# Strassen's scheme for three quarters of an MLP's first product, on one core

## The chip, the core and the metric

The kernel runs on one core of a Trainium2 chip. The core has a matrix engine (TensorE, PE in the profile; PEld is its loading of weights), three engines for elementwise work (VectorE = DVE, ScalarE = ACT, GpSimd = POOL), and SyncE (SP), whose queue issues the DMAs here. Each engine has its own queue of instructions, and semaphores order the work between them. SBUF is the memory that the engines work in, PSUM the one that TensorE writes its products to. The metric is the device time of one execution in microseconds (us); lower is better. Every number below is from the profile of one execution or from the times of the runs.

## The reference

One layer of a decoder: attention and a gated linear recurrence beside each other, merged, then an MLP with a squared ReLU. It is computed for 512 prompt tokens and 64 sample tokens (8 requests of 8), which share the weights; together 576 columns. The part that the change rewrites is the MLP, with D_MODEL = 1024 and D_FF = 4096:

```python
u2 = x1 * (1 + sc2) + sh2
hid = jnp.square(jax.nn.relu(jnp.einsum('bsd,df->bsf', u2, w_up) + b_up))
ff = jnp.einsum('bsf,fd->bsd', hid, w_down) + b_down
x2 = _layer_norm(DN_ALPHA * x1 + g2 * ff, ln2_g, ln2_b, dtype)
```

Everything is float32. The sample tokens have a scale and shift (`sc2`, `sh2`) for each request, the prompt has one.

## The kernel before

**Precision.** TensorE multiplies in a reduced format (fp32r). Each float32 operand is therefore split into a high part, rounded to fp32r by an ACT copy, and a low part, the DVE difference; a product is three matmuls: high by high, high by low, low by high.

**Layout.** Activations lie transposed: 8 pages of 128 channels by 576 columns each. The columns go in two halves of `HF` = 288, each a matmul's moving operand. A block is 128 output channels: for each half, 8 steps of k by 3 terms, so 2 x 24 = 48 matmuls into one PSUM bank per half (`half`, line 1780, with `mm_part`, line 382), then the eviction of that bank.

**Weights.** A unit is 1024 rows by 512 columns (4 blocks) or 256 columns (2 blocks). `load_one` (line 307) loads it in pieces of 1 MB into three raw buffers (`NRAW`); a buffer is handed on by `weights_done`. `split_slot` (line 372) makes the high and low parts of one block, in instructions of 128 x 512: an ACT copy to `whi` and a DVE subtraction to `wlo` for each piece. Token-major units (the values of the attention, the last product of the MLP) are split by rows of k instead, in `split_k` (line 355), 512 columns at a time.

**Pages.** Nearly all of SBUF is one pool of `NPG` = 68 pages of 128 x 576 floats. Activations, weight parts, caches and temporaries all take pages; a page comes free when the last instruction that touches it has run.

**Order.** The program is straight-line. `tc.manual_schedule()` (line 252) leaves each engine the order in which the Python code issues its instructions. `Side` (line 177) interleaves generators of side work ("lanes") with the matmuls: each `pump` runs a step if its lane is ready by the kernel's own planner (`Engine`, line 109).

**The stages.** The front (until about 905 us) computes projections, attention, the recurrence and the branches. Then come the output product with the first layer norm, then the MLP in four quarters of 1024 of the 4096 hidden channels: 8 up blocks (`up_evac`, line 1765: ACT adds the bias and takes the ReLU, POOL squares, ACT writes the high part `hdh`, DVE the low part `hdl`) and 8 down blocks (`down_evac`, line 1805: added into `acc`). The list `seq` (line 1818) holds them in order; quarter 0's first four up blocks run ahead of it beside the layer norm. The loop over `seq` (line 1866) splits the weights of block i + 1, may issue a copy of cache rows (`copy_rows`), then runs block i. In quarter 0's down blocks ACT also scales the residual `hT`; in quarter 2's the sum is added to `hT` (`gated`). Quarter 3 has no down blocks in `seq`: its down product is made token-major by `blocks` and `tiles` (lines 1968 and 1992), after eight `split_k` at the last block. `residual` (line 1843) transposes gates and residual for that stage beside quarter 3's up blocks.

The lines of the loop around which the change is made:

```python
        if i + 1 < len(seq):
            split(*seq[i + 1][:2])
        else:
            for k in range(AHEAD_K):
                split_k(ud[0], k)
        if i >= 8:
            copy_rows()
        for h in range(2):
            half(u, j, xs, h, ev)
```

Of the kernel before, what the change touches and what calls it, by code (L numbers as in the profile page):

```python
# [19 lines left out]
KT = D // 128  # L20
# [31 lines left out]
NPG = 68  # L52
AHEAD_K = 8
# [190 lines left out]
def decoder_step(ctx, tc, I, O):  # L244
# [3 lines left out]
    raw = ctx.enter_context(tc.tile_pool(name="raw", bufs=NRAW))  # L248
    small = ctx.enter_context(tc.tile_pool(name="small", bufs=2))
# [12 lines left out]
    def page(shape, name, dtype=F32):  # L262
        return pages.tile(shape, dtype, name=name, tag="page")

# [72 lines left out]
    def split(u, j):  # L337


        def there():  # L340
            load_more(True)
            return len(u["slots"]) > j // 5 if u["tok"] else loaded(u)
        if not there():
            side.drain(("a", "s"), there)
        assert there()
        if u["tok"]:
            for k in range(j // 5 * 4, j // 5 * 4 + 4):
                split_k(u, k)
            return
        for s in range(len(u["slots"])):  # L350
            split_slot(u, j, s)
        if j == len(u["blocks"]) - 1:
            weights_done(u["slots"])

    def split_k(u, k, eng=V):

        if k in u["w"]:
            return
        load_more(True)
        t = u["slots"][k // 4][2][:, k % 4]  # L360
        w = u["w"][k] = page([128, 512], "whi", F32R), page([128, 512], "wlo", F32R)
        A.activation(w[0], t, AF.Copy)
        eng.tensor_sub(w[1], t, w[0])
        if k % 4 == 3:
            weights_done(u["slots"][k // 4:k // 4 + 1])
# [6 lines left out]
    def split_slot(u, j, s):  # L372
        k0, kk, t = u["slots"][s]
        hi, lo = u["w"].setdefault(j, ([], []))
        for k in range(0, kk, 4):
            src = t[:, k:k + 4, j * 128:(j + 1) * 128]
            hi.append(page([128, 4, 128], "whi", F32R))
            lo.append(page([128, 4, 128], "wlo", F32R))
            A.activation(hi[-1], src, AF.Copy)
            V.tensor_sub(lo[-1], src, hi[-1])  # L380

    def mm_part(w, nk, xs, h, ps, ks):
        hi, lo = w
        seq = [(hi, 0), (hi, 1), (lo, 0)]
        n = 0
        for k in ks:
            for m, (ww, xi) in enumerate(seq):
                PE.matmul(ps, ww[k // 4][:, k % 4], xs[xi][k][:, h * HF:(h + 1) * HF],
                          start=(k == 0 and m == 0), stop=(k == nk - 1 and m == 2))
                n += 1  # L390
                if n % 8 == 0 and n < 3 * len(ks):
                    side.pump(8 * 123.0)
# [1101 lines left out]
    for qd in range(4):  # L1494
        for n0 in (0, 4):
            unit(I["w_up"][0], 0, 8, (qd * 8 + n0) * 128, 512, [None] * 4)
        for n0 in (0, 4) if qd < 3 else (4, 0, 4):
            unit(I["w_down"][0], qd * 1024, 8, n0 * 128, 512, [None] * 4, tok=(qd == 3))
    for u in units:
        for k0 in range(0, u["nk"], 2048 // u["W"]):  # L1500
            load_q.append((u, k0))
# [83 lines left out]
    for j in range(n_early):  # L1585
        done_split.add((id(u0), j))
        split_slot(u0, j, 0)
# [3 lines left out]
    for s in range(4):  # L1591
# [13 lines left out]
        if s == 1:  # L1605
            for j in range(n_early):
                split_slot(u0, j, 1)
# [197 lines left out]
    def down_evac(qd, n):  # L1805
        def evac(hf, ps):
            if qd == 0:
# [3 lines left out]
                A.activation(hv(hT[n], hf), hv(hT[n], hf), AF.Identity, scale=gbl[:, 0, n:n + 1], bias=gbl[:, 1, n:n + 1])  # L1811
            else:
                V.tensor_add(hv(acc[n], hf), ps, hv(acc[n], hf))
                if qd == 2:
                    gated(hT[n], hv(acc[n], hf), hf, 5, n)
        return evac

    seq = []
    for qd in range(4):
        for n in range(8):  # L1820
            if qd == 0 and n < 4:
                continue
            seq.append((mlp[qd * 4 + n // 4], n % 4, U2, up_evac(qd, n)))
        if qd < 3:
            for n in range(8):
                seq.append((mlp[qd * 4 + 2 + n // 4], n % 4, (Hd[0], Hd[1]), down_evac(qd, n)))
# [16 lines left out]
    def residual():  # L1843
# [11 lines left out]
        for c in range(NM // 128):  # L1855
            for e in range(2):
# [5 lines left out]
                yield 436, None  # L1862

    n_down = len(seq) - 8
    ud = mlp[14:17]
    for i, (u, j, xs, ev) in enumerate(seq):
# [4 lines left out]
        if i == n_down:  # L1871
            side.add("p", residual())
        if i + 1 < len(seq):
            split(*seq[i + 1][:2])
        else:
            for k in range(AHEAD_K):
                split_k(ud[0], k)
        if i >= 8:
            copy_rows()
        for h in range(2):  # L1880
            half(u, j, xs, h, ev)
        u["w"].pop(j)
    side.drain()
    U2_hi[:] = U2_lo[:] = [None] * 8
# [83 lines left out]
    def blocks(w, e):  # L1968
        for n in range(4):
            ps = bank([128, NT - NM], "lin")  # L1970
            for k in range(KT):
                if n == 0 and k + AHEAD_K < KT:
                    split_k(w, k + AHEAD_K)
# [11 lines left out]
    def pass_on(u, k, v):  # L1985
# [3 lines left out]
        if k >= KT - AHEAD_K:  # L1989
            split_k(v, k - KT + AHEAD_K)  # L1990

    def tiles(w, e):
        for c in range(NM // 128):
            last = c == NM // 128 - 1

            def before(k):
                if w is ud[1]:
                    if last and k >= 2:
                        w["w"].pop(k - 2)
                    if k % 2 == SPH:  # L2000
                        split_k(ud[2], 4 * c + k // 2, V if c else G)
# [13 lines left out]
    blocks(ud[1], 0)  # L2015
    tiles(ud[1], 0)
# [38 lines left out]
```

## Time and profile before

| | us |
|---|---|
| median of 3 runs (lowest to highest) | 1381.82 (1379.16 to 1386.65) |
| the profiled execution | 1381.52 |
| its span, first to last instruction | 1379.7 |
| quarter 0's down blocks, in the trace | 1000 to 1053 |
| quarter 1: up blocks, down blocks | 1053 to 1104, 1104 to 1155 |
| quarter 2: up blocks, down blocks | 1155 to 1205, 1205 to 1256 |
| quarter 3's up blocks | 1256 to 1309 |
| its down product and the end | 1309 to 1380 |

In rows of groups, a name such as `wlo<-wraw,whi` is the tile written and the tiles read; after it stand the shapes. A time in brackets after a row of the timeline is the idle time of that engine ahead of it, with what ended it. All instructions carry line 173, that of the helper which issues them, so tiles tell them apart. A row of the windows gives, for a stretch of the span, its length, the busy time of each engine with its instructions, the granted clock of TensorE (1.00 is full), the DMA's share and its GB/s.

### The profile page before, as it was taken

The numbers are of one execution on the slowest core, as the hardware profiler recorded it, in microseconds if no ns is written. First come the engines' busy times: TensorE is split into PE (matmuls) and PEld (weight loads), VectorE is DVE, ScalarE is ACT, GpSimd is POOL, SyncE is SP. The second block draws the span as 40 slices with busy tenths as digits, with TensorE's granted clock in tenths as the row PEclk, the third lists the DMA queues.
The fourth block names the chain that finished last, engine by engine and source line by source line (L and its number), as shares of the span: only waits on it lengthen the run. The fifth ranks groups of instructions, "written<-read, shape, count | busy, mean of one in ns | idle before, by whom it ended". The sixth has DMA issues, their size and how long they took to land.

```text
span 1379.7 us, 24690 instructions
## 1 busy us (share of the span) xinstructions
PE 1330.6 (96%) x9624; PEld 1228.2 (89%) x9624; DVE 766.6 (56%) x1572; ACT 469.5 (34%) x1101; POOL 359.9 (26%) x419
## 2 busy tenths in 40 slices
PE   6999999999899999999999999999999999999995
PEld 3899898799778887888899999998999999999994
DVE  2456555558767886566655446547522333354458
ACT  3423333332422232333233441325554422413522
POOL 1242023026417563234344200003500200200205
PEclk9999999999999999999999999999999999999998
DMA  9789899689989977776445223331123633522322
GB/s 295 255 306 341 268 317 339 238 272 324 280 282 285 319 243 242 240 239 199 147 157 170 70 73 112 130 123 62 62 107 129 237 124 147 220 77 91 118 99 69
DMA packets 184520, 269.40 MB, mean 195 GB/s; under 512 B 15756, under 2 KB 92372, under 8 KB 183892
## 3 DMA queue, kind: packets, MB, share of 16 engines
q1 hardware_dynamic: 184404, 267.83, 57.7%
q8 instruction: 76, 1.25, 0.4%
q14 instruction: 40, 0.33, 0.1%
HBM read 210.45 MB, written 74.10 MB: 206 GB/s over the span
## 4 chain that ended last, share of the span: by engine, by line
PE 83%; DVE 6%; DMA 4%; ACT 2%; issue 2%; POOL 2%; SPq 1%; DVEq 0%; POOLq 0%; ACTq 0%
PE lin L173 68%; PE att L173 7%; PE tr L173 4%; PE sx L173 4%; DVE wlo L173 2%; DMA out_dram<-kv 2%; DVE res L173 1%; DMA kv<-in_cache_kv_w_dram 1%; POOL qb L173 1%; ACT whi L173 1%; SPq L173 1%; DMA xtm<-in_x_prompt_dram 0%; DMA wraw<-in_w_ada_dram 0%; DMA qb<-qsc 0%; DVE st L173 0%
## 5 line engine op out<-in xcount | busy, mean ns | idle before, releaser
L173 DVE TENSOR_TENSOR wlo<-wraw,whi 128x512 fp32r<-128x512 f32 x340 | 248.4, 774 | 128.5 <-ACT whi L173 125.7
L173 PE MATMUL lin<-uh,whi 128*128 128x288 f32 x992 | 298.4, 301 | 4.3 <-DVE hso L173 2.4
L173 PE MATMUL lin<-uh,wlo 128*128 128x288 f32 x992 | 298.2, 301 | 2.3 <-DVE wlo L173 2.3
L173 PE MATMUL lin<-ul,whi 128*128 128x288 f32 x992 | 299.3, 302 | 1.0 <-DVE ul L173 0.9
L173 ACT ACTIVATE whi<-wraw 128x512 fp32r<-128x512 f32 x344 | 193.4, 620 | 112.8 <-DMA wraw<-in_w_down_dram 29.7
L173 PEld LDWEIGHTS lin<-ul,whi 128*128 128x128 f32 x992 | 187.6, 189 | 13.7 <-issue 10.9
L173 PEld LDWEIGHTS lin<-uh,whi 128*128 128x128 f32 x992 | 187.5, 189 | 10.3 <-DVE hso L173 2.7
L173 PEld LDWEIGHTS lin<-uh,wlo 128*128 128x128 f32 x992 | 187.7, 189 | 7.1 <-issue 3.8
L173 POOL TENSOR_TENSOR qb<-qb,kv 128x512 f32<-128x512 f32 x96 | 128.3, 1356 | 204.0 <-DMA qb<-qsc 90.7
L173 PE MATMUL lin<-u2h,whi 128*128 128x288 f32 x496 | 147.1, 297 | 1.2 <-ACT u2h L173 1.2
L173 PE MATMUL lin<-u2l,whi 128*128 128x288 f32 x496 | 147.0, 296 | 0.3 <-DVE u2l L173 0.3
L173 PE MATMUL lin<-u2h,wlo 128*128 128x288 f32 x496 | 146.8, 296 | 0.0
L173 PE MATMUL lin<-hdh,whi 128*128 128x288 f32 (+1 forms) x448 | 133.6, 298 | 0.2 <-ACT hdh L173 0.2
L173 PE MATMUL lin<-hdl,whi 128*128 128x288 f32 (+1 forms) x448 | 132.9, 297 | 0.1
L173 PE MATMUL lin<-hdh,wlo 128*128 128x288 f32 (+1 forms) x448 | 133.0, 297 | 0.0
L173 POOL TENSOR_TENSOR rel<-rel 128x288 f32<-128x288 f32 x56 | 38.3, 684 | 292.7 <-ACT rel L173 287.7
L173 PEld LDWEIGHTS lin<-u2h,whi 128*128 128x128 f32 x496 | 93.4, 188 | 1.8 <-ACT u2h L173 1.5
L173 PEld LDWEIGHTS lin<-u2l,whi 128*128 128x128 f32 x496 | 93.3, 188 | 1.5 <-DVE u2l L173 0.9
L173 DVE TENSOR_TENSOR hdl<-rel,hdh 128x288 fp32r<-128x288 f32 x61 | 28.4, 466 | 118.5 <-ACT hdh L173 118.5
L173 PEld LDWEIGHTS lin<-u2h,wlo 128*128 128x128 f32 x496 | 93.3, 188 | 0.5 <-issue 0.5
L173 PEld LDWEIGHTS lin<-hdh,whi 128*128 128x128 f32 x448 | 84.1, 188 | 0.7 <-ACT hdh L173 0.4
L173 PEld LDWEIGHTS lin<-hdl,whi 128*128 128x128 f32 x448 | 84.1, 188 | 0.3 <-DVE hdl L173 0.3
(358 smaller groups left out, 2546.6 us busy)
## 6 DMA issues: line engine op xcount, KB each, us to landing
wraw<-in_w_in_dram SPq DMA_DIRECT2D x42, 1024.0 KB
kv<-in_cache_kv_w_dram SPq DMA_DIRECT2D x144, 256.0 KB
qb<-qsc SPq DMA_DIRECT2D x96, 256.0 KB
wraw<-in_w_down_dram SPq DMA_DIRECT2D x18, 1024.0 KB
out_dram<-kv SPq DMA_DIRECT2D x64, 256.0 KB
wraw<-in_w_ada_dram SPq DMA_DIRECT2D x16, 1024.0 KB
wraw<-in_w_up_dram SPq DMA_DIRECT2D x16, 1024.0 KB
out_dram<-in_cache_kv_w_dram SPq DMA_DIRECT2D x32, 512.0 KB
```

The lines of the kernel that those rows point to most:

```text
L173: return f(out, *args, **kw)
```

## The change

A unit of `w_up` (1024 rows by 512 columns) is taken as 2 x 2 blocks A11, A21, A12, A22 of 512 rows by 256 columns, and the input u2 as 2 x 2 blocks of 512 channels by 288 columns. Strassen's scheme, in Winograd's form, makes the product from seven products of such blocks or of sums of them, in place of eight. This is done in quarters 1, 2 and 3; quarter 0's up blocks and all down blocks stay as they are.

- `input_sums` makes the sums of the inputs and their high and low parts once, as side work beside quarter 0's down blocks; it also stores `hT` to DRAM (`xsc`) and gives up its pages. `reload` brings `hT` back beside quarter 2's down blocks, where its scaling now stands too.
- `seven` gives a unit's seven products as pairs of `prep(f)` (the sum of weights on DVE, in place in the raw buffer, for four of them; a high part on ACT and a low part on DVE, each of 128 x 1024) and `run(f)` (two column groups of 12 matmuls, the eviction with bias or the DVE addition of an earlier sum, and, from the fourth product on, ReLU, square and the parts of one quarter of the unit's outputs). Three pairs of PSUM banks change roles from unit to unit. The square of these quarters is ACT's, no longer POOL's.
- The loop calls `prep` for entry i + 2 ahead of `run` for entry i. `seq` has 70 entries: 4 up blocks and 8 down blocks, then twice 14 products and 8 down blocks, then 14 products.
- The pool has 59 pages, and a second pool six tiles of 4 KB per partition for weight parts (`wpart`): a block's high and low part are one tile each, and `split_k` takes two rows of k in one instruction there (the first six of a token unit's eight). The first three units after the front still use pages.
- `residual` runs after the loop, beside `blocks`, and the eight `split_k` for the last product are spread over four of the loop's last five entries.

```diff
-NPG = 68
-AHEAD_K = 8
+NPG = 59
+NWP = 6
...
+    def wpart(shape, name, dtype=F32R):
+
+        return parts.tile(shape, dtype, name=name, tag="part")
...
+        k -= k % 2
+        t = u["slots"][k // 4][2][:, k % 4:k % 4 + 2]
+        hi, lo = wpart([128, 2, 512], "whi"), wpart([128, 2, 512], "wlo")
+        A.activation(hi, t, AF.Copy)
+        eng.tensor_sub(lo, t, hi)
...
+    def split_rows(u, j, src, hi, lo):
+        A.activation(hi, src, AF.Copy)
+        V.tensor_sub(lo, src, hi)
...
+            V.tensor_sub(b11, b12, b11)
+            V.tensor_sub(b12, b22, b12)
+            V.tensor_sub(b22, b22, b11)
+            V.tensor_sub(b21, b21, b22)
...
+                a11, a21, a12, a22 = (st["A"] + [None] * 2)[:4]
+                src = (a11, a21, a11, a12, a21, a12, a22)[f]
+                if f == 1:
+                    V.tensor_add(a21, a21, a22)
+                elif f == 2:
+                    V.tensor_sub(a11, a21, a11)
+                elif f == 4:
+                    V.tensor_sub(a21, a22, a11)
+                elif f == 5:
+                    V.tensor_sub(a12, a12, a11)
+                forms[f] = hi, lo = wpart([128, 4, 256], "whi"), wpart([128, 4, 256], "wlo")
+                A.activation(hi, src, AF.Copy)
+                V.tensor_sub(lo, src, hi)
+                if f >= 5:
+                    weights_done(u["slots"][f - 5:f - 4])
...
+                hi, lo = forms[f]
+                nm = "acabaca"[f]
+                for p in range(2):
+                    if f in (0, 1, 3):
+                        st[nm].append(bank([128, HF], st[nm][0]))
+                    ps = st[nm][1 + p]
+                    for k in range(4):
+                        for m, (ww, xi) in enumerate(((hi, 0), (hi, 1), (lo, 0))):
+                            PE.matmul(ps, ww[:, k, p * 128:(p + 1) * 128], X[f][xi][k], start=(f in (0, 1, 3) and k == 0 and m == 0),
+                                      stop=(k == 3 and m == 2), skip_group_check=True)
+                    b1, b2 = (vcol(V_BUP, qd * 8 + n0 + 2 * i + p) for i in range(2))
+                    if f < 3:
+                        if not p:
+                            st[f] = page([128, NT], "sn")
+                        A.activation(hv(st[f], p), ps, AF.Identity, bias=b2 if f == 1 else b1)
+                    elif f < 6:
+                        x = hv(st[(0, 1, 2)[f - 3]], p)
+                        V.tensor_add(x, ps, x)
+                    else:
+                        if not p:
+                            st[6] = page([128, NT], "sn")
+                        A.activation(hv(st[6], p), ps, AF.Relu, bias=b2)
+                    side.pump(12 * 133.0)
+                if f >= 3:
+                    x = st[(0, 1, 2, 6)[f - 3]]
+                    if f < 6:
+                        A.activation(x, x, AF.Relu)
+                    A.activation(x, x, AF.Square)
+                    finish(x, n0 + (0, 2, 0, 2)[f - 3], (0, 1, 1, 0)[f - 3])
...
+        if i + 2 < len(seq):
+            seq[i + 2][0]()
+
+        for k in {5: (0, 1), 4: (2, 3), 2: (4, 5), 1: (6, 7)}.get(len(seq) - i, ()):
+            split_k(ud[0], k, two=False)
+        if i >= 6 and i % 2 == 0:
             copy_rows()
...
+        run()
     side.drain()
+    side.add("a", residual(list(hT)))
```

`finish(x, n, h)` writes, for two hidden pages n and n + 1 and half h, the high part by an ACT copy and the low part by a DVE subtraction, 288 columns each.

More of the change, by code (lines that the diff above doesn't have):

```diff
@@ L347, in split, with split_k @@
             for k in range(j // 5 * 4, j // 5 * 4 + 4):
-                split_k(u, k)
+                split_k(u, k, two=(k < 6))
             return
-        for s in range(len(u["slots"])):
-            split_slot(u, j, s)
+        split_block(u, j, four=u.get("four", False))
         if j == len(u["blocks"]) - 1:
             weights_done(u["slots"])
-    def split_k(u, k, eng=V):
+    def split_k(u, k, eng=V, two=True):
         if k in u["w"]:
@@ L359, in split_k @@
         load_more(True)
[L360 to L364, printed above, removed]
+        if not two:
+            t = u["slots"][k // 4][2][:, k % 4]
+            w = u["w"][k] = page([128, 512], "whi", F32R), page([128, 512], "wlo", F32R)
+            A.activation(w[0], t, AF.Copy)
+            eng.tensor_sub(w[1], t, w[0])
+            if k % 4 == 3:
+                weights_done(u["slots"][k // 4:k // 4 + 1])
+            return
+        k -= k % 2
[3 more added lines that the diff above has]
+        eng.tensor_sub(lo, t, hi)
+        for i in range(2):
+            u["w"][k + i] = hi[:, i], lo[:, i]
+        if k % 4 == 2:
             weights_done(u["slots"][k // 4:k // 4 + 1])
@@ L370, in split_once, with split_block @@
             split(u, j)
[L372 to L380, printed above, removed]
+    def split_block(u, j, slots=None, four=False):
+        if j not in u["w"]:
+            u["w"][j] = [], []
+            if not four:
+                u["home", j] = tuple(wpart([128, u["nk"], 128], nm) for nm in ("whi", "wlo"))
+        for k0, kk, t in u["slots"] if slots is None else [u["slots"][s] for s in slots]:
+            src = t[:, :, j * 128:(j + 1) * 128]
+            if four:
+                for k in range(0, kk, 4):
+                    split_rows(u, j, src[:, k:k + 4], *(page([128, 4, 128], nm, F32R) for nm in ("whi", "wlo")))
+            else:
+                split_rows(u, j, src, *(t[:, k0:k0 + kk] for t in u["home", j]))
+    def split_rows(u, j, src, hi, lo):
+        A.activation(hi, src, AF.Copy)
+        V.tensor_sub(lo, src, hi)
+        for k in range(src.shape[1]):
+            for part, t in zip(u["w"][j], (hi, lo)):
+                part.append(t[:, k])
     def mm_part(w, nk, xs, h, ps, ks):
@@ L1498, in decoder_step @@
             unit(I["w_down"][0], qd * 1024, 8, n0 * 128, 512, [None] * 4, tok=(qd == 3))
+    for u in units[n_front:n_front + 3]:
+        u["four"] = True
     for u in units:
@@ L1818, in decoder_step, with plain, run, reload @@
+    def plain(u, j, xs, evac):
+        def run():
+            for h in range(2):
+                half(u, j, xs, h, evac)
+            u["w"].pop(j)
+        return [(lambda: split_once(u, j), run)]
+    ud = mlp[14:17]
+    def reload(n):
+        hT[n] = page([128, NT], "hT")
+        SP.dma_start(hT[n], xsc[n])
     seq = []
@@ L1841, in decoder_step, with residual @@
     R = [[None, None] for _ in range(5)]
-    def residual():
+    def residual(hT):
         for e in range(2):
@@ L1862, in residual @@
                 yield 436, None
-    n_down = len(seq) - 8
-    ud = mlp[14:17]
-    for i, (u, j, xs, ev) in enumerate(seq):
+        gate.append(True)
+    n_down = len(seq) - 22
+    seq[0][0]()
+    seq[1][0]()
+    for i, (_, run) in enumerate(seq):
         if i < 4:
@@ L1870, in decoder_step @@
                     G.tensor_mul(hv(hT[k], h), hv(hT[k], h), rstds[h])
[L1871 to L1878, printed above, removed]
+        if i == 4:
+            side.add("p", input_sums())
+        if i == 12:
+            side.drain()
+        if n_down <= i < n_down + 8:
+            if i == n_down:
+                side.flush(True)
+                reload(0)
+            if i < n_down + 7:
+                reload(i - n_down + 1)
+        if i + 2 < len(seq):
[3 more added lines that the diff above has]
+        if i >= 6 and i % 2 == 0:
             copy_rows()
-        for h in range(2):
-            half(u, j, xs, h, ev)
-        u["w"].pop(j)
+        run()
     side.drain()
+    side.add("a", residual(list(hT)))
     U2_hi[:] = U2_lo[:] = [None] * 8
@@ L2015, in decoder_step @@
     blocks(ud[1], 0)
+    side.drain(until=lambda: len(gate) > 2)
     tiles(ud[1], 0)
```

87 lines of the change are left out of this document (76 added, 11 removed).

## The prediction

> **What bounds the kernel now.** I read the page's sums first, then its chain, then windows by stage, then single rows.
>
> ```profile
> PE 1330.6 (96%) x9624; PEld 1228.2 (89%) x9624; DVE 766.6 (56%) x1572; ACT 469.5 (34%) x1101; POOL 359.9 (26%) x419
> PE 83%; DVE 6%; DMA 4%; ACT 2%; issue 2%; POOL 2%; SPq 1%; DVEq 0%; POOLq 0%; ACTq 0%
> ```
>
> TensorE is busy for 96% of the span and makes 83% of the chain. The MLP's loop (the list `seq`) is the extreme of it. The windows below are quarter 0's down blocks, then up, down and up blocks of quarter 1 and 2 and quarter 2's down blocks; after them a piece of the chain (start, length, what).
>
> ```profile
> core 0: us, PE busy (x) PEld busy (x) DVE busy (x) ACT busy (x) POOL busy (x), PEclk, DMA share, GB/s
> 1000.00:1053.00 53.00, 53.00 (x402) 53.00 (x401) 11.44 (x19) 26.52 (x53) 1.61 (x3) 1.00 0.39 149
> 1053.00:1104.00 51.00, 51.00 (x387) 51.00 (x386) 17.16 (x32) 22.90 (x48) 10.67 (x16) 1.00 0.43 166
> 1104.00:1155.00 51.00, 51.00 (x387) 51.00 (x386) 18.59 (x35) 9.68 (x18) 0.00 (x0) 1.00 0.44 166
> 1205.00:1256.00 51.00, 51.00 (x387) 51.00 (x386) 27.86 (x65) 10.04 (x19) 0.25 (x1) 1.00 0.29 103
> ...
> 1049.99 209.08 PE lin L173 x1578
> ```
>
> In 209 us PE never waits: 209.08 / 1578 = 0.1325 us for each matmul of 288 columns, at clock 1.00. A block of 48 takes 6.36 us. DVE and ACT have 17 to 23 of 51 us to do. So matmuls taken out here come off the end, as long as the other engines go on feeding PE.
>
> **What the change removes.** Quarters 1 to 3 have 24 up blocks of 48 matmuls, 1152 in all. A unit of four blocks becomes seven products of 24, 168 for 192. That removes 6 x 24 = 144 matmuls, 144 x 0.1325 = **19.1 us**, if nothing waits. A product lasts 3.18 us, a unit 22.26 (25.44 before).
>
> **What it adds on ACT and DVE.** Rows (ns as min/median/max; then busy us and mean ns, for the two 576-column forms):
>
> ```profile
> L173 ACT ACTIVATE whi<-wraw x128: 611/616/634, 970.0 to 1350.1; 128x512 fp32r<-128x512 f32 x128
> L173 DVE TENSOR_TENSOR wlo<-wraw,whi x124: 675/686/1775, 970.6 to 1361.2; 128x512 fp32r<-128x512 f32 x124
> L173 ACT ACTIVATE hdh<-rel x61: 443/445/447, 961.0 to 1311.4; 128x288 fp32r<-128x288 f32 x61
> L173 DVE TENSOR_TENSOR hdl<-rel,hdh x61: 457/459/575, 961.4 to 1311.9; 128x288 fp32r<-128x288 f32 x61
> L173 ACT ACTIVATE rel<-lin,vT x59: 480/502/504, 960.0 to 1310.1; 128x288 f32<-128x288 f32 x59
> L173 DVE TENSOR_TENSOR acc<-lin,acc x32: 451/458/459, 1105.7 to 1254.9; 128x288 f32<-128x288 f32 x32
> ...
> L173 DVE TENSOR_TENSOR hgl<-hg,hgh 128x576 fp32r<-128x576 f32 x8 | 6.0, 752 | 0.0
> ...
> L173 ACT ACTIVATE hgh<-hg 128x576 fp32r<-128x576 f32 x8 | 5.4, 674 | 0.0
> ```
>
> The new instructions of 1024 columns are in no row. Below they can't be shorter than those of 576 (ACT 0.674, DVE 0.752); above they are bounded by two of 512 in a row (1.14 and 1.30, rows below). The line through 288 and 576 columns gives ACT 1.03 and DVE 1.21; I take these, since 512 lies on it within 0.01 (DVE) and 0.01 (ACT).
> A unit then needs on DVE 11 of 1024 (four sums of weights, seven low parts), six additions from PSUM and eight low parts: 13.3 + 2.7 + 3.7 = 19.7 us. ACT: seven of 1024, eight evictions, seven of 576, eight of 288: 7.2 + 4.0 + 4.7 + 3.6 = 19.5. Either sum is below 22.26. What decides is the order.
>
> ```profile
> 1072.07 1.14 ACT L173 ACTIVATE whi<-wraw 128x512 fp32r<-128x512 f32 x2
> ...
> 1072.72 1.30 DVE L173 TENSOR_TENSOR wlo<-wraw,whi 128x512 fp32r<-128x512 f32 x2
> ...
> 974.38 0.45 ACT L173 ACTIVATE rel<-rel 128x288 f32<-128x288 f32 x1
> 974.85 0.45 ACT L173 ACTIVATE hdh<-rel 128x288 fp32r<-128x288 f32 x1
> ...
> 984.74 0.48 ACT L173 ACTIVATE rel<-lin,vT 128x288 f32<-128x288 f32 x1
> 988.15 0.44 ACT L173 ACTIVATE hdh<-rel 128x288 fp32r<-128x288 f32 x1 [2.93 <-POOL rel L173]
> 988.50 0.49 ACT L173 ACTIVATE rel<-lin,vT 128x288 f32<-128x288 f32 x1
> ```
>
> Read here: each engine keeps the order of the program (ACT stands 2.93 us before `hdh`, with the next `rel` behind it); an engine that waits for another starts 0.03 us after it (whi's first ends at 1072.69, wlo begins at 1072.72); independent instructions overlap by 0.09 (ACT, 1.14 for twice 0.616) and 0.08 (DVE); a dependent one on ACT starts 0.03 after the end (974.38 + 0.45, then 974.85).
>
> **The loop between ACT and DVE.** `prep(f+2)` stands ahead of `run(f)`. So for the products f = 3, 4, 5 DVE holds: low part of f+2, two additions of f, two hidden low parts; ACT holds: high part of f+2, relu, square, two hidden high parts of f, then the high part of f+3. The low part waits for the high part, the additions are queued behind that low part, relu waits for the second addition, and the next high part is queued behind it all. One turn: 1.03 + 0.03 (hi), 1.13 (lo until the first addition), 0.38 + 0.46 + 0.03 (additions), 0.70 + 0.71 (relu, square), 0.36 + 0.36 (copies) = **5.2 us, where PE needs 3.18**. At the lower bounds it is 4.4, still longer.
> The other turns, from high part to high part by the same rows: f = 5 of one unit to f = 6, and 6 to 0 of the next, 5.2 each; 0 to 1: 7.0 (a sum of weights stands behind the last hidden low part: + 1.7); 1 to 2: 5.1; 2 to 3: 1.8; 3 to 4 and 4 to 5: 3.45 each (high, low, sum). A lap is **31 us** against PE's 22.3.
> Put on a clock with 0 at the start of a quarter's first product: its high parts of f = 2 to 5 start at 1.8, 3.8, 7.2, 10.7, early enough; f = 6 at 15.9. The second unit's start at 21.1, 28.0 (PE wants it ready at 25.4), 33.1, 34.9, 38.3, 41.8, 47.0; then ACT splits two down blocks at 52.2 and 57.1, and behind the second it evicts, squares and copies the last product: evictions 58.1, square 59.05, copy 59.8, low part of `Hd[6]` from 60.2 to 60.7. PE, unhindered, wants that page 18 matmuls into the first down block, at 44.52 + 18 x 0.1325 = 46.9. A quarter loses 60.2 - 46.9 + 0.4 = **13.7 us**: some 8 in the second unit, 5 at the first down block. At the lower bounds it loses 6.2, at the upper 16.2. In quarter 3 four splits for the last product of the MLP (ACT 2.1, DVE 2.5 us) stand in the same loop: 15.9 (8.1 to 18.4). Sum 2 x 13.7 + 15.9 = **43.3** (20.5 to 50.8).
>
> **The clock.**
>
> ```profile
> 326.00:329.00 3.00, 1.16 (x15) 0.96 (x15) 3.00 (x5) 0.49 (x1) 2.69 (x3) 1.00 0.84 229
> 329.00:332.40 3.40, 3.40 (x17) 3.40 (x17) 1.71 (x6) 0.74 (x3) 2.55 (x3) 0.50 1.05 401
> ...
> 368.00:371.00 3.00, 2.68 (x12) 1.88 (x10) 2.90 (x4) 0.82 (x2) 2.54 (x2) 1.00 1.03 367
> 371.00:375.00 4.00, 3.01 (x16) 2.53 (x17) 2.78 (x8) 0.98 (x2) 0.13 (x1) 1.00 1.11 298
> ```
>
> After 1.84 us without matmuls (3.00 - 1.16) the granted clock is 0.50 for 3.4 us; after 1.3 in the second pair it stays. Half of 3.4 is 1.7 us. In the second unit such a stretch lies inside the waits for ACT and costs nothing; behind the 4.6 us stall at the first down block PE is the bound again: 1.5 each, three times, **4.5** (0 to 8).
>
> **Front.** Weights leave the pages for three pairs of 4 KB tiles; a block used four pages or eight, so 59 is about what the rest had. Non-token blocks are split one block ahead, 6 us of cover. Token groups aren't: two rows of k now come as one instruction.
>
> ```profile
> 77.67 2.18 ACT L173 ACTIVATE whi<-wraw 128x512 fp32r<-128x512 f32 x4
> ...
> 78.33 4.94 DVE L173 TENSOR_TENSOR wlo<-wraw,whi 128x512 fp32r<-128x512 f32 x4 [15.99 <-ACT whi L173]
> ...
> 81.01 0.62 PE L173 MATMUL lin<-wlo,uh 128*128 128x512 f32 x1 [0.60 <-DVE wlo L173]
> 82.72 0.63 PE L173 MATMUL lin<-wlo,uh 128*128 128x512 f32 x1 [0.62 <-DVE wlo L173]
> ```
>
> PE already waits for the low parts of a token unit's second half. As pairs the first comes 0.9 us later or more, of which the second gives some back: 0 to 1.2 for each of five units, **3** (-3 to +8, with the effect of other page counts, which I can't trace).
>
> **At nothing.** Quarter 0's sums of inputs (32 subtractions of 288 columns and 16 small ones on DVE, 12 us on ACT) lie beside its down blocks, where DVE has 42 and ACT 26 of 53 us free; without that cover 3 us. The scaling of `hT` moves from there to quarter 2's down blocks, with ACT 41 of 51 free. POOL loses 48 squares that ended no chain. SP gets eight stores and reloads of 0.3 MB and spreads its copies; a weight load waits in SP's queue for the last reader (10.7 + 1.2 and 18.1 on the clock above) and is wanted at 28; 1 MB at that stage's 166 GB/s takes 6.3. `residual` moves its 24 transposes to the next stage, also PE's.
>
> **Sum**, against the profiled execution's 1381.5 (span 1379.7 and 1.8 around it; the median of the runs is 1381.8): - 19.1 + 43.3 + 4.5 + 3 = + 31.7, **1413**.
>
> **Rivals.**
> (1) *PE stays the bound, faster.* The two products of lead, 6.4 us, and the slack of the sums (19.7 and 19.5 of 22.26) carry the loop. It decides if a turn is under 3.18 us, or a lap under 22.3. Then - 19.1 + 3 = 1365. For it: 209 us without a wait, and both sums. Against it: the order on the queues, and 4.4 us a turn even at the lower bounds. 0.11. The Trainium skill (Perfetto Trace Analysis, Identifying the Most-Contended Engine) says the same in general: find the engine with the highest occupancy and improve that one. By it the removed matmuls come off the end; the trace agrees on who is busiest, but its rows of waits show ACT standing still in order.
> (2) *The loop is real but light.* Instructions of 1024 columns cost hardly more than those of 576: - 19.1 + 20.5 = + 1.4, 1383, with no clock loss; it decides under 0.75 us each. Against it: DVE and ACT rows grow linearly from 288 to 576. 0.06.
> (3) *More waits than the loop*: the pages run short in the front or in quarter 2 with `hT` reloaded, each token unit pays a half-clock stretch too (5 x 1.7), and the loop costs its upper bound: + 31.7 + 7.5 + 8.5 = 1429 or more. For it: the first token unit already waits twice. 0.10.
>
> **Numbers.** The forecast has 0.73. The range goes from 1393 (the loop at seven tenths, no clock loss, front at nothing) to 1430 (the loop at its upper bound, clock and front at 8 each); it leaves out rivals 1 and 2. Half a per cent, 7 us, is about what a measurement tells from no change: faster 0.11, same 0.06, slower 0.83.
>
> **What would show it.** Right: PE idle in the up stages of quarters 1 to 3, waiting for `whi`, then `wlo`, in the second unit of each and for `hdh` at the first down block; starts of ACT's high parts some 5.2 us apart there; clock 0.50 behind the gap; DVE additions waiting for no one, late behind `wlo`. The first unit of each quarter without waits. Wrong: PE at 51 of 51 us in these stages, or `whi` of 1024 columns under 0.75 us; or another order of the queues, with additions ahead of low parts. A changed front (before 900 us) of over 8 us would be a term that I don't have.

## The result and the profile after

| | before | after |
|---|---|---|
| median, us (lowest to highest) | 1382.22 (1379.16 to 1386.65) | 1422.99 (1418.98 to 1423.72) |
| ratio after / before, 95% interval | | **1.0285** (1.0255 to 1.0314) |
| profiled execution; its span, us | 1381.52; 1379.7 | 1423.38; 1421.6 |

The changed kernel is 2.9% slower. The page's sums first: busy time of each engine, then the chain's shares.

```profile
PE 1336.2 (94%) x9480; PEld 1226.2 (86%) x9480; DVE 831.6 (58%) x1591; ACT 513.1 (36%) x1078; POOL 327.8 (23%) x371
PE 64%; DVE 10%; ACT 8%; DMA 4%; issue 3%; SPq 1%; POOL 1%; DVEq 0%; ACTq 0%; POOLq 0%
```

PE has its 144 matmuls fewer (9480 for 9624) and is still the busiest engine by far, but its share of the chain fell from 83% to 64%, and that of DVE and ACT together rose from 8% to 18%. The busy sums don't tell why: DVE went from 56% to 58%. The next table splits the span by the start of each stage's first matmul in the trace, in us; the last column is the prediction's sum, taken apart by stage (a quarter: -6.4 removed, 13.7 loop, 1.5 clock).

| stage | before | after | difference | predicted |
|---|---|---|---|---|
| until the first projection | 23.2 | 23.6 | +0.5 | } |
| projections, attention, recurrence | 787.2 | 793.9 | +6.7 | } +3 |
| branches, output product | 131.1 | 131.3 | +0.1 | } |
| quarter 0, up | 58.8 | 61.3 | +2.6 | } |
| quarter 0, down | 50.9 | 50.9 | 0 | 0 |
| quarter 1, up and down | 101.8 | 111.0 | +9.2 | +8.8 |
| quarter 2, up and down | 101.8 | 111.9 | +10.1 | +8.8 |
| quarter 3, up, and the first half of the last product | 85.4 | 98.3 | +12.9 | +11.0 |
| to the end | 39.7 | 39.4 | -0.2 | 0 |
| sum | 1379.7 | 1421.6 | +41.9 | +31.7 |

The windows of after (busy time and instructions by engine, granted clock, DMA): quarter 0's down blocks, then up and down blocks of quarters 1 and 2, then quarter 3's up blocks.

```profile
1010.00:1061.00 51.00, 51.00 (x387) 51.00 (x386) 28.74 (x66) 27.79 (x56) 1.96 (x4) 1.00 0.48 169
1061.00:1114.40 53.40, 47.54 (x339) 46.27 (x338) 31.31 (x42) 31.60 (x52) 0.00 (x0) 0.97 0.32 114
1114.40:1172.00 57.60, 53.23 (x387) 52.55 (x386) 22.75 (x40) 14.58 (x26) 0.00 (x0) 0.97 0.38 142
1172.00:1227.00 55.00, 48.53 (x339) 47.15 (x337) 33.63 (x46) 31.33 (x51) 0.00 (x0) 0.94 0.35 125
1227.00:1284.00 57.00, 54.08 (x386) 53.64 (x386) 30.49 (x66) 22.78 (x41) 0.00 (x0) 0.94 0.45 171
1284.00:1346.00 62.00, 50.28 (x338) 48.53 (x336) 38.77 (x57) 36.81 (x63) 0.00 (x0) 0.90 0.41 144
```

Quarter 0's down blocks hide the sums of the inputs wholly (51.00 of 51). In every later up stage PE stands for some 6 to 12 us, and the clock is granted at 0.90 to 0.97. DVE and ACT are busy for only 31 of 53 us there, and yet they set the time. The timeline of ACT, and then of DVE, in quarter 1 of after shows how; a number in brackets is the idle time ahead of a row and what ended it.

```profile
1071.86 1.06 ACT L173 ACTIVATE whi<-wraw 128x1024 fp32r<-128x1024 f32 x1 [0.62 <-DVE wraw L173]
1074.94 1.40 ACT L173 ACTIVATE sn<-sn 128x576 f32<-128x576 f32 x2 [2.02 <-DVE sn L173]
1076.37 0.78 ACT L173 ACTIVATE hdh<-sn 128x288 fp32r<-128x288 f32 x2
1077.06 1.05 ACT L173 ACTIVATE whi<-wraw 128x1024 fp32r<-128x1024 f32 x1
1080.13 1.41 ACT L173 ACTIVATE sn<-sn 128x576 f32<-128x576 f32 x2 [2.02 <-DVE sn L173]
1081.57 0.78 ACT L173 ACTIVATE hdh<-sn 128x288 fp32r<-128x288 f32 x2
1082.25 1.05 ACT L173 ACTIVATE whi<-wraw 128x1024 fp32r<-128x1024 f32 x1
```
```profile
1072.95 1.23 DVE L173 TENSOR_TENSOR wlo<-wraw,whi 128x1024 fp32r<-128x1024 f32 x1 [1.19 <-ACT whi L173]
1074.09 0.81 DVE L173 TENSOR_TENSOR sn<-att,sn 128x288 f32<-128x288 f32 x2
1076.85 0.83 DVE L173 TENSOR_TENSOR hdl<-sn,hdh 128x288 fp32r<-128x288 f32 x2 [1.94 <-ACT hdh L173]
1078.14 1.23 DVE L173 TENSOR_TENSOR wlo<-wraw,whi 128x1024 fp32r<-128x1024 f32 x1 [0.46 <-ACT whi L173]
1079.28 0.81 DVE L173 TENSOR_TENSOR sn<-sx,sn 128x288 f32<-128x288 f32 x2
```

Read the two together, by start times. ACT makes a high part at 1071.86; DVE takes the low part of it at 1072.95 and only then the two additions of the product that PE has finished (1074.09); ACT stands for 2.02 us until they are done, takes the ReLU and the square, copies, and reaches the next high part at 1077.06. One turn is 1077.06 - 1071.86 = 5.20 us, the next 1082.25 - 1077.06 = 5.19, where PE has 3.18 us of matmuls. Each engine waits for the other in turn, so neither is ever full. PE's stalls in quarter 1, the largest of the second unit and the one inside the first down block:

```profile
1090.79 0.40 PE L173 MATMUL sx<-u2h,whi 128*128 128x288 f32 x1 [3.01 <-ACT sn L173]
...
1121.47 0.40 PE L173 MATMUL lin<-hdh,whi 128*128 128x288 f32 x1 [4.21 <-ACT hdh L173]
```

### The profile page after: what moved, and what is told of

The parts are those of the page before. It is cut to its first block, busy times and chain, and to the rows that moved or that the text cites. A ratio compares the mean times of both kernels' runs of the same rounds, so it can differ in the third digit from the quotient of the medians.

```text
span 1421.6 us, 24368 instructions
## 1 busy us (share of the span) xinstructions
PE 1336.2 (94%) x9480; PEld 1226.2 (86%) x9480; DVE 831.6 (58%) x1591; ACT 513.1 (36%) x1078; POOL 327.8 (23%) x371
## 4 chain that ended last, share of the span: by engine, by line
PE 64%; DVE 10%; ACT 8%; DMA 4%; issue 3%; SPq 1%; POOL 1%; DVEq 0%; ACTq 0%; POOLq 0%
PE lin L173 51%; PE att L173 6%; DVE wlo L173 4%; ACT whi L173 3%; PE sx L173 3%; PE tr L173 3%; ACT sn L173 3%; DVE wraw L173 2%; DMA out_dram<-kv 2%; DMA qb<-qsc 1%; ACT hdh L173 1%; DVE sn L173 1%; DVE res L173 1%; SPq L173 1%; DMA wraw<-in_w_in_dram 1%
## 5 line engine op out<-in xcount | busy, mean ns | idle before, releaser
L173 DVE TENSOR_TENSOR wlo<-wraw,whi 128x512 fp32r<-128x512 f32 (+1 forms) x251 | 261.4, 1065 | 163.9 <-ACT whi L173 162.2
L173 ACT ACTIVATE whi<-wraw 128x512 fp32r<-128x512 f32 (+1 forms) x255 | 204.0, 832 | 171.7 <-PE lin L173 86.0
L173 POOL TENSOR_TENSOR wlo<-wraw,whi 128x512 fp32r<-128x512 f32 x4 | 6.4, 1601 | 373.5 <-ACT whi L173 373.5
L173 PEld LDWEIGHTS lin<-hdh,wlo 128*128 128x128 f32 x448 | 86.8, 194 | 0.3 <-DVE wlo L173 0.3
L173 PE MATMUL lin<-whi,uh 128*128 128x512 f32 x160 | 68.4, 428 | 1.1 <-DVE kT L173 0.7
L173 PE MATMUL lin<-wlo,uh 128*128 128x512 f32 x160 | 64.0, 400 | 1.3 <-DVE wlo L173 1.3
L173 DVE TENSOR_REDUCE sc<-qb 128x4 f32<-128x512 f32 x96 | 63.4, 677 | 0.8 <-POOL qb L173 0.6
L173 PE MATMUL lin<-whi,ul 128*128 128x512 f32 x160 | 63.1, 394 | 0.0
L173 PE MATMUL lin<-u2h,whi 128*128 128x288 f32 x176 | 54.4, 309 | 4.8 <-ACT sn L173 3.0
L173 POOL TENSOR_TENSOR hk<-hk,T 128x256 f32<-128x256 f32 (+1 forms) x48 | 41.1, 856 | 76.5 <-PE tr L173 41.6
```

Of the source, the lines that this page charges most:

```text
L173: return f(out, *args, **kw)
```

## The experiments

Theory A, from the prediction: the order of the low part and the additions on DVE makes a loop of ACT and DVE that is slower than PE. Rivals: the instructions themselves are too many (B), or the loss comes from pages, tiles, loads or the clock and not from the scheme (C). The first four kernels described below ran beside 25 runs of the kernel before (median 1383.62 us); sums_ahead, best and best_halves ran on the same chip beside 25 others (1384.35); best2 ran on another chip beside 11 (1384.21). The ratios are against these, that of after against the four runs of the result.

| kernel | median, us | ratio, 95% | quarter 1 | quarter 2 | quarter 3 and first half of the last product | front to the output product | quarter 0, up |
|---|---|---|---|---|---|---|---|
| before | | | 101.8 | 101.8 | 85.4 | 941.5 | 58.8 |
| after | 1422.99 | 1.0285 | 111.0 | 111.9 | 98.3 | 948.8 | 61.3 |
| adds_first | 1390.84 | 1.0046 (1.0027 to 1.0064) | 100.2 | 100.3 | 91.6 | 949.2 | 59.6 |
| no_relu_square | 1380.08 | 0.9974 (0.9951 to 0.9998) | 97.1 | 97.1 | 86.1 | 948.2 | 61.4 |
| plain | 1388.31 | 1.0028 (1.0008 to 1.0048) | 101.8 | 101.8 | 85.1 | 944.6 | 61.4 |
| before_64 | 1401.77 | 1.0123 (1.0079 to 1.0168) | 101.8 | 101.8 | 85.4 | 963.9 | 58.8 |
| sums_ahead | 1381.05 | 0.9987 (0.9971 to 1.0003) | 97.0 | 97.0 | 87.2 | 948.8 | 59.7 |
| best | 1375.79 | 0.9944 (0.9923 to 0.9966) | 95.4 | 95.4 | 85.4 | 948.3 | 61.3 |
| best_halves | 1383.39 | 1.0002 (0.9987 to 1.0018) | 95.4 | 95.4 | 84.0 | 956.6 | 59.6 |
| best2 | 1373.92 | **0.9928** (0.9905 to 0.9951) | 95.4 | 95.4 | 81.4 | 948.5 | 61.3 |

The stage columns are of one profiled execution each, cut as in the table above, in us. By the removed matmuls alone a quarter would be 101.8 - 48 x 0.1325 = 95.4.

**adds_first: the additions ahead of the low part.**

```diff
                 A.activation(hi, src, AF.Copy)
-                V.tensor_sub(lo, src, hi)
+                def low():
+                    V.tensor_sub(lo, src, hi)
+                late.append(low)
...
                 if f >= 3:
+                    lows()
                     x = st[(0, 1, 2, 6)[f - 3]]
```

The whole splits of the down blocks are put behind in the same way.

> In this version the two DVE additions of a product stand ahead of the low part of the product two entries on; every instruction and every duration stays. Theory A (the order on the two queues makes a loop between ACT and DVE, 5.2 us a turn in the products 3 to 5): the turn there falls below PE's 3.18 us, since ReLU no longer waits for a low part. By the same rows a quarter then loses 4.8 us in place of 13.7, the last one 10.5 in place of 16.9: 24 us less, some 2 to 4 more by fewer half-clock stretches, so 1396 us (1390 to 1402). The sums of weights behind the last hidden low parts still make PE wait some 3 us in the second unit. Theory B (DVE and ACT simply have too much to do in these stages, 20 of 22 us a unit with gaps): the same work in another order takes the same time, 1423 (1418 to 1427). Theory C (the time is lost to the clock and to DMA, the waits are a sign of it): no change either.

Measured 1390.84 us, 32 under after, by a change of order alone. The kernel has every instruction that after has. A quarter takes 100.2 us, 4.8 over its matmuls, which is the figure expected. DVE in quarter 1 of adds_first:

```profile
1078.42 0.83 DVE L173 TENSOR_TENSOR hdl<-sn,hdh 128x288 fp32r<-128x288 f32 x2 [0.82 <-ACT hdh L173]
1079.16 0.81 DVE L173 TENSOR_TENSOR sn<-lin,sn 128x288 f32<-128x288 f32 x2
1079.89 1.21 DVE L173 TENSOR_TENSOR wlo<-wraw,whi 128x1024 fp32r<-128x1024 f32 x1
```

The additions (`sn`) now follow without a wait, and the low part behind them doesn't either. So the order was most of the loss (A); the number of instructions (B) and pages or loads (C) can't have been that, since both are unchanged.

**no_relu_square: two of ACT's instructions taken out of the loop.** The ReLU and the square of quarters 1 to 3 are left out (of the seventh product, its square).

```diff
-                    if f < 6:
-                        A.activation(x, x, AF.Relu)
-                    A.activation(x, x, AF.Square)
```

> Leaves out the ReLU of 576 columns and the square of the hidden units in quarters 1 to 3 (the ReLU in the last product's eviction stays): 42 ACT instructions of 576 columns, 0.68 us each, 28 us of ACT in all. Theory A: the turn shrinks by 1.4 to 3.8 us, a quarter loses 3.8 us in place of 13.7, the last one 7 in place of 16.9: 30 us less and fewer half-clock stretches, 1392 us (1386 to 1398). Theory B with DVE as the full engine (19.7 of 22.26 us a unit): DVE has the same to do, 1420 (1415 to 1425). Theory C: no change.

Measured 1380.08, 12 us under what was expected and below the range given. The direction agrees with the loop (a turn shortened on ACT, with DVE's order as in after, frees PE too). The size doesn't. Two things make most of the miss, by the stages of the profiles. Quarters 1 and 2 take 97.1 us each where the working on a clock gave 99.2, so it overrates what stalls remain in a shorter loop (4.2 us). And those of after lie 4.7 us above the 109.1 that the loop alone would make (95.4 + 13.7), which goes too; behind its stalls stand the stretches at half clock, for which little was taken off.

**plain: the rest of the change without the scheme.** All quarters go by blocks of 48 matmuls; the tiles of 4 KB, 59 pages, the two-row splits and `residual`'s place stay; the sums of the inputs and the reload of `hT` go with the scheme, POOL squares again, and the copies of cache rows are spaced as before.

```diff
-            if qd == 0:
-                seq += plain(mlp[1], n % 4, U2, up_evac(0, n))
-            elif n % 4 == 0:
-                seq += seven(mlp[qd * 4 + n // 4], qd, n)
+            seq += plain(mlp[qd * 4 + n // 4], n % 4, U2, up_evac(qd, n))
```

> The changed kernel with the eight up blocks of quarters 1 to 3 made as before, without Strassen's scheme, the sums of inputs and the store and reload of hT; the pages, the weight tiles, the token units' pairs of rows, splitting two entries ahead and the later residual stay. Theory A: the up and down stages take 50.9 us again without waits of PE, and what is left is the longer front: 1382 + 7 (projections) + 2.6 (first up blocks) = 1391 to 1392 us. If the front is longer because of what comes after it (its planner or its loads), it is as before: 1382. If the weight tiles themselves cost the MLP something, it is over 1395.

Measured 1388.31, 4.7 us over the 25 runs of the kernel before, where 9.6 (7 + 2.6) were expected. The stages of quarters 1 and 2 are those of before; both windows of plain are full:

```profile
1060.00:1111.00 51.00, 51.00 (x387) 51.00 (x386) 17.13 (x32) 23.47 (x48) 10.67 (x16) 1.00 0.43 166
1111.00:1162.00 51.00, 51.00 (x387) 51.00 (x386) 18.11 (x33) 9.27 (x16) 0.00 (x0) 1.00 0.43 165
```

So the scheme carries the loss of the quarters; what else was changed carries 4.7 us, ahead of them, in the projections (+2.9 in the profile) and quarter 0 (+2.6).

**before_64: the kernel before with 64 pages for 68.** One number, `NPG`, is changed.

> The kernel before with 64 pages in place of 68, nothing else. It asks whether the longer front of the changed kernel is for want of pages. If pages are scarce in the front, four fewer make it longer by 5 us or more: 1387 us or more. If they are not, 1382 within 3 us. In the changed kernel the front has 55 to 59 pages beside its weight tiles, in this one 48 to 56 beside its weights.

Measured 1401.77, and all of it (963.9 - 941.5 = 22.4 us in the profile) in the front. Pages are dear there: four of them, 6% of the pool, cost 18 us of the median. The change paid for its tiles with nine pages that no longer held weights, and came off far cheaper than that.

**sums_ahead: the sums of weights one entry earlier.** What adds_first still lost sat where a sum of weights of 1.22 us stood ahead of a high part.

```diff
     def lows():
         while late:
             late.pop(0)()
+        if ahead:
+            ahead.pop()()
...
             seq[i + 2][0]()
+        if i + 3 < len(seq):
+            ahead.append(seq[i + 3][3])
```

> As adds_first, and the sum of weights of the form after next is made on DVE one entry earlier, behind the low part of the next form, so that ACT's high part finds it ready. The result is still whole. Theory A (what is left in adds_first, 4.8 us a quarter over the matmuls' own time and some 9 in quarter 3, is for the greater part ACT and then the low part waiting behind a sum of weights of 1.22 us): a quarter falls from 100.2 to 97.4 us, quarter 3 by about 4, together 9 to 10 us under adds_first, 1382 us (1378 to 1386). Rival (what is left is the first block of the down stage, which reads the last hidden pages, and the clock): quarters stay at 100 and the time at 1388 to 1393.

Measured 1381.05, 9.8 under adds_first and one under expectation. Quarter 1's up stage of sums_ahead has no stall left; what is over is in its down stage:

```profile
1059.50:1104.20 44.70, 44.70 (x339) 44.70 (x339) 31.72 (x44) 33.52 (x56) 0.00 (x0) 1.00 0.42 154
1104.20:1156.60 52.40, 51.36 (x385) 50.91 (x384) 22.02 (x37) 12.48 (x24) 0.00 (x0) 1.00 0.37 142
```

Set beside after: DVE and ACT do 31.7 and 33.5 us of work in this stage, as they did in after (31.3 and 31.6), and PE is full. **The work was never too much, only its order.**

**best: the first down block takes its later half first, and the last splits are spread otherwise.**

```diff
-    def plain(u, j, xs, evac):
+    def plain(u, j, xs, evac, hs=(0, 1)):
...
-            for h in range(2):
+            for h in hs:
...
-                seq += plain(mlp[qd * 4 + 2 + n // 4], n % 4, (Hd[0], Hd[1]), down_evac(qd, n))
+                seq += plain(mlp[qd * 4 + 2 + n // 4], n % 4, (Hd[0], Hd[1]), down_evac(qd, n), (0, 1) if qd == 0 or n else (1, 0))
...
-        for k in {5: (0, 1), 4: (2, 3), 2: (4, 5), 1: (6, 7)}.get(len(seq) - i, ()):
+        for k in {6: (0, 1), 5: (2,), 2: (3, 4), 1: (5, 6, 7)}.get(len(seq) - i, ()):
```

> As sums_ahead, and two edits more: in quarters 1 and 2 the first block of the down stage takes its second half of columns first, so that the pages of the last form are read 3 us later; and the eight splits of the last quarter's down weights are spread otherwise over the last six entries, two and one ahead of the last forms and five behind them. Theory A: no stall is left at the down stage of quarters 1 and 2 (1.2 to 1.8 us each) and quarter 3 loses about 2 us less: 5 us under sums_ahead, 1377 us (1373 to 1381), so that the scheme beats the kernel before by 0.1 to 0.7%. Rival (the stall only moves to the next block, or the clock gives the gain back): the time of sums_ahead within 2 us.

Measured 1375.79, 5.3 under sums_ahead, where 5 were expected; 0.56% under the kernel before. Quarters 1 and 2 now cost PE's matmuls and nothing else (95.4). Windows of best: quarter 1, up and down; then quarter 3's up stage, the stall behind it, and the stage after that.

```profile
1060.50:1105.20 44.70, 44.70 (x340) 44.70 (x339) 31.71 (x44) 33.48 (x56) 0.00 (x0) 1.00 0.41 155
1105.20:1156.10 50.90, 50.90 (x387) 50.90 (x386) 22.03 (x37) 12.57 (x24) 0.00 (x0) 1.00 0.38 144
1251.40:1296.10 44.70, 44.68 (x337) 44.44 (x336) 34.61 (x51) 33.18 (x55) 0.00 (x0) 1.00 0.39 137
1296.10:1300.30 4.20, 0.15 (x1) 0.15 (x1) 2.42 (x5) 4.14 (x9) 0.00 (x0) 0.89 1.10 427
1300.30:1337.00 36.70, 36.22 (x239) 35.84 (x240) 16.48 (x48) 13.30 (x33) 0.30 (x1) 0.92 0.26 87
```

The whole gain of quarter 3 is lost in the two last rows: 4.07 us of stall, then a clock of 0.92 on average, from 6.8 us at half speed.

**best2: the first two blocks of the last product interleaved**, in banks that the last product of the scheme doesn't hold.

```diff
+        first = [bank([128, NT - NM], t) for t in ("sx", "att")] if w is ud[0] else []
+        order = [(n, range(KT)) for n in range(4)]
+        if first:
+            order[0:2] = [(n, ks) for ks in (range(0, 4), range(4, 6), range(6, 8)) for n in (0, 1)]
```

> As best, and the first two blocks of the last down stage are taken together: hidden pages 0 to 3 for both, then 4 and 5 for both, then 6 and 7 for both, into PSUM banks that the last form doesn't use. In best, TensorE stands 4.07 us at 1296.08 ahead of this stage, for the bank that ACT empties at 1300, and two stretches of half clock (6.8 us) follow. Theory G (a stall costs its own length and then half of the stretch at half clock behind it): both go, and the time is 4.1 + 3.4 = 7.5 us under best, 1368.5 us (1365 to 1372). Rival G0 (the stretches at half clock come anyway): 4 us less, 1372 us. Rival H (the stall only moves on, to the last hidden pages, which are ready at 1302.5): within 1.5 us of best, 1375 us.

Windows of best2, cut at the same starts as the last three of best:

```profile
1251.40:1296.10 44.70, 44.70 (x340) 44.70 (x338) 34.63 (x51) 33.02 (x54) 0.00 (x0) 1.00 0.38 136
1296.10:1300.30 4.20, 4.20 (x31) 4.20 (x30) 2.23 (x5) 4.11 (x9) 0.00 (x0) 1.00 1.13 442
1300.30:1333.10 32.80, 30.05 (x211) 28.87 (x210) 16.74 (x47) 13.46 (x33) 0.23 (x1) 1.00 0.29 97
```

Stall and half clock are gone, as theory G said, and the stage ends 3.8 us sooner in the profile, not 7.5: PE is idle for 2.75 of the 32.8 us behind (in best 0.48 of 36.7), in shorter waits, the longest, 1.61 us, ahead of a transpose. These make 2.3 of the 3.7 us that are missing; the rest was not traced. The median is 1373.92, 1.9 under best, with overlapping intervals and on another chip: between G0 and H. So theory G holds for the stall and the half clock behind it, and not for the time. Against the kernel before it is the best that was run, 0.72% faster.

**best_halves: low parts of 512 columns in the plain blocks.** This asks about the front.

```diff
-        V.tensor_sub(lo, src, hi)
+        for k in range(0, src.shape[1], 4):
+            V.tensor_sub(lo[:, k:k + 4], src[:, k:k + 4], hi[:, k:k + 4])
```

> As best, and the low parts of the blocks of the plain scheme are made by DVE instructions of 512 columns again, two in place of one of 1024; tiles, pages and loads stay. Theory F1 (the front and quarter 0 lost their 9.3 us of the profiles because a DVE instruction of 1024 columns holds its high part's readers up, the one of 8.96 us at 439 above all): the wait of 4.84 us at 442 goes and projections with quarter 0 take 3 to 6 us less than in best, 1373 us. Theory F2 (the front lost them to weight loads that come later, six tiles of 4 KB and fewer pages, and the length of an instruction is no matter): the same as best, or up to 3 us more for some 250 further DVE instructions.

Measured 1383.39, 7.6 over best, more than either theory allowed; the front grew by 8.3 us. F1 falls: the wait of 4.84 us was to go, and PE still stands there for 4.32. Its one great instance, the low part at 439 us, in after first and then in best_halves (durations in ns, min/median/max):

```profile
L173 DVE TENSOR_TENSOR wlo<-wraw,whi x1: 8958/8958/8958, 439.5 to 439.5; 128x1024 fp32r<-128x1024 f32 x1
```
```profile
L173 DVE TENSOR_TENSOR wlo<-wraw,whi x2: 1759/5094/8428, 439.4 to 447.7; 128x512 fp32r<-128x512 f32 x2
```

Here one instruction of 512 columns alone took 8.43 us, against 0.68 elsewhere: its length is not the reason. F2 isn't shown either. In the trace the longer front has a new wait of PE of 5.99 us at 594.8 for ACT's `moda`, in all 3.6 us more idle PE, and 33.8 us at half clock in the projections for best's 20.2. What brought these on stays open.

## Why the prediction was right, and where it was off

The forecast was 1413 in 1393 to 1430; the median is 1422.99, inside, and slower as said. By the profile the loss is 41.9 us for the 31.7 of the sum. Of these 10.2 us the front makes 6.8, quarter 3 1.9 and quarter 2 1.3.

**Removed matmuls.** Right: 144 fewer, and where nothing waits (best) a quarter is shorter by 101.8 - 95.4 = 6.4, the 6.36 of the prediction.

**Durations.** Right. Rows of after by form (busy us, mean ns):

```profile
L173 DVE TENSOR_TENSOR wlo<-wraw,whi 128x1024 fp32r<-128x1024 f32 x41 | 50.2, 1225 | 36.9 <-ACT whi L173 36.9
L173 ACT ACTIVATE whi<-wraw 128x1024 fp32r<-128x1024 f32 x40 | 42.2, 1056 | 58.2 <-DVE wraw L173 48.8 <-PE lin L173 9.4
```

1.225 and 1.056 us where 1.21 and 1.03 were taken. So rival 2, which needed under 0.75, is out.

**The loop.** Right in mechanism and size. Turns of 5.20 and 5.19 against 5.2; ACT's high parts of quarter 1 start at 1071.86 and, one unit later, at 1103.11, a lap of 31.25 against 31. Loss and clock together: 111.0 - 95.4 = 15.6 in quarter 1 and 16.5 in quarter 2, against 13.7 + 1.5 = 15.2. The loop's part can be read alone: PE goes on in the first down block at 1121.47 and 1232.45, 60.45 and 60.48 us after the first matmul of its quarter (1061.02, 1171.97). Without waits that would be 46.9, so 13.6 us are lost by then in either, where 13.7 were taken. This includes the half clock inside the second unit, which so costs nothing of its own, as said. Not as said: no wait of PE in quarter 1 is put down to `whi`. They end with `wlo` (0.72 and 0.34 us), with DVE's addition (1.70) and, the largest (3.01), with ACT's eviction of the seventh product, which frees the PSUM bank `sx`. The eviction stands behind a high part that waits for its sum of weights, so it is the same queue, one instruction later. ACT in after:

```profile
1089.29 1.06 ACT L173 ACTIVATE whi<-wraw 128x1024 fp32r<-128x1024 f32 x1 [1.75 <-DVE wraw L173]
1090.25 0.87 ACT L173 ACTIVATE sn<-sx,vT 128x288 f32<-128x288 f32 x2
```

adds_first shows that the order makes it, and sums_ahead that the rest of it was order too.

**Rival 1 and the busiest engine.** Rival 1 (PE stays the bound) failed in after, and then came true in quarters 1 and 2 of best, by changes of order alone. What spoke for it, the sums of work, 19.7 and 19.5 of 22.26 us, does fit; the condition that decided was the turn, 5.2 us against 3.18. The case shows that fitting sums are not enough. Of rival 3 the longer front came true, the loop at its upper bound did not.

**The clock.** The mechanism was right and the size small. The stall in the first down block, or in quarter 3 ahead of the last product, came with 3.4, 6.8 and 6.8 us of half clock in quarters 1, 2 and 3. Some 0.9 and 1.7 us of the last two lie inside the stall, so the cost is 1.7, 3.0 and 2.6 us where 1.5 was taken.

**At nothing.** Right: quarter 0's down blocks are full, with the sums of inputs beside them. One reading behind it was wrong, without weight: POOL's squares did end a chain. In before's chain POOL's `rel` stands with 2.7 us between 1302.6 and 1311.4, ahead of the last product, but PE itself stood there for only 0.17 us (at 1311.89).

**The front is the term that was mis-sized:** 3 taken (-3 to +8), 9.8 in the profile with quarter 0's up blocks. The two-row splits of the token units, from which the 3 was drawn, show no loss at the place where they were read; PE's waits there, in after, for 0.60 and 0.62 before:

```profile
81.25 0.63 PE L173 MATMUL lin<-wlo,uh 128*128 128x512 f32 x1 [0.41 <-DVE wlo L173]
...
84.65 0.63 PE L173 MATMUL lin<-wlo,uh 128*128 128x512 f32 x1 [0.60 <-DVE wlo L173]
```

Three other things do. First, at 443.7 us PE stands for 4.84 us, for the low part of 8.96 us (before: 2.28 us at 452, behind another instruction, below). Second, at 478 PE stands for 4.12 us. Third, the stretches at half clock are longer. PE's rows of after:

```profile
448.54 0.61 PE L173 MATMUL lin<-uh,wlo 128*128 128x288 f32 x1 [4.84 <-DVE wlo L173]
```
```profile
482.34 1.11 PE L173 MATMUL sx<-ident,moda 128*128 128x128 f32 x4 [4.12 <-ACT moda L173]
```

The second is followed back on ACT, in after:

```profile
477.32 1.06 ACT L173 ACTIVATE whi<-wraw 128x1024 fp32r<-128x1024 f32 x1 [7.34 <-DMA wraw<-in_w_in_dram]
481.34 0.46 ACT L173 ACTIVATE q<-hq 128x288 f32<-128x288 f32 x1 [2.96 <-DVE hq L173]
481.70 0.58 ACT L173 ACTIVATE moda<-sx 128x512 f32<-128x512 f32 x1
```

ACT waits 7.34 us for a weight load, and `moda`, which PE wants, is queued behind. SP issued this load at 469.7; in before the load that comes at this place was issued at 462.0, and ACT waited 0.40 us for it. It is a wait of an in-order queue again. plain, which has the tiles and pages of after without the scheme, has it too (4.0 us), so the scheme isn't its cause. Other waits became shorter: over the projections after has 25.6 us of idle PE for before's 21.7, and 23.5 us at half clock for 17.1. That is 3.9 + 6.4 / 2 = 7.1, about the difference of 6.7. Why the load is issued later (fewer tiles for weights, or the planner's order) was not settled: kernels with 57 pages and seven tiles, or with pages for all blocks, were not run. The front also varies: plain has the same code there and took 790.1 for projections where after took 793.9. The 2.6 us of quarter 0's up blocks are taken up at the end of the last section.

## What to carry to other kernels

When two engines with in-order queues hand work to each other, add up the turn from one instruction to its successor along both queues and compare it with the bound engine's time; shares of 60% on both say nothing against a loop that is too slow. If the sums fit and the turn doesn't, reorder first: put what the other engine waits for ahead of what only the next turn needs, and make inputs a turn earlier; here that was worth 47 us with the same work done. Behind a stall of a few us ask for two prices, the stall and the slow clock behind it, and expect shorter waits to show up where the long one was.

## What the runs showed of the hardware

**A DVE instruction can be held up beside a run of POOL instructions.** In the kernel before it is `hf`, with POOL's row from the same time:

```profile
444.98 8.39 DVE L173 TENSOR_SCALAR hf<-hf,lbt 128x576 f32<-128x576 f32 x1
```
```profile
441.83 11.22 POOL L173 TENSOR_TENSOR qb<-qb,kv 128x512 f32<-128x512 f32 x9
```

`hk`, of the same form, takes 0.52 us on average in that profile; `hf` ended 0.3 us after the POOL run did (453.37 and 453.05). In after it is the low part at 439.52, beside seven such POOL products from 439.97; it ended at 448.48, 1.1 us before they did. In the other seven kernels that were read for it, all with 4 KB tiles, this low part took 7.7 to 10.2 us (the first of best_halves' two, 8.4). So the hold was there before the change; which instruction falls into it, and who waits for that, goes with the order. That POOL is the cause is read from the times alone, since no run moved its products. But of the 340 low parts of the kernel before, none of the 268 with POOL idle for nine tenths of its time or more took over 0.4 us beyond the median, and 22 of the 38 with POOL busy for over nine tenths did. The Trainium skill (GPSIMD Engine Reference, 1. Specifications) lists the memory interfaces of that engine as shared with VectorE, with contention for DVE instructions that have two inputs there or run in a two-port mode; the rows of the low part, which has two, agree; whether `hf` counts among them no run here shows.

**Half clock comes in pieces of 3.4 us: none, one or two of them, behind the same gap.** PE's gap ahead of quarter 0's second half of columns, in before and then in after, with the windows that follow each:

```profile
959.25 0.40 PE L173 MATMUL lin<-u2h,whi 128*128 128x288 f32 x1 [1.24 <-ACT u2h L173]
...
960.50:963.90 3.40, 3.40 (x14) 3.19 (x14) 2.46 (x7) 1.53 (x4) 3.08 (x9) 0.50 0.00 0
```
```profile
966.60 0.40 PE L173 MATMUL lin<-u2h,whi 128*128 128x288 f32 x1 [1.25 <-ACT u2h L173]
...
968.80:975.60 6.80, 6.23 (x26) 5.88 (x26) 6.80 (x13) 1.86 (x4) 6.20 (x10) 0.50 0.00 0
```

Gaps of 1.24 and 1.25 us; half clock for 3.4 and for 6.8. The gap is 1.24 to 1.25 us in all ten traces, and the change doesn't settle what follows: best has 6.8 too, sums_ahead 3.4, adds_first and best_halves none. Quarter 0's up blocks take 59.6 to 59.7 us in the changed kernels with none or one piece, 61.3 to 61.4 in those with two. So 1.7 us of the 2.6 which they lost go with the second piece; the rest is about the length of two waits of PE that before hasn't (0.57 us at 970.49 for `u2l`, 0.49 at 990.94 for `rel`). In each of the ten traces all these stretches start whole steps of 3.413 us apart; in after those at 1091.64, 1122.36, 1200.87 and 1231.59 us are 9, 23 and 9 steps apart. So where in a step the gap falls may decide how many pieces follow; no run tested that. The Trainium skill (TensorE: Matmul & The Clock Gate, What's actually happening) has a window of 3413 ns that runs freely, and the slow clock after at least one idle window; the length and the even steps agree with the traces. A gap of 1.25 us with half clock behind it doesn't fit an idle window of 3.4 us, and here the measurement decides.
